# Hymba block (mLSTM and sparse attention heads) on one core: order of weight sums, gate evaluation, paced transposes and a block-by-block ending

## The chip, the cores and the metric

One Trainium2 core of a chip, one launch. The metric is device microseconds of that core. The engines: TensorE (PE, with its weight loads as PEld), VectorE (DVE), ScalarE (ACT), GpSimd (POOL) and the queue of SyncE (SP), which issues the loads of weights.

## What is computed

A batch of 256 tokens with 4096 features goes through one block in float32:

```
h = rmsnorm(x);  u = h @ w_in                       # 4096 x 15424
y_ml = rmsnorm(mlstm(conv(q,k), v, i, f)) * sigmoid(o) * silu(z)     # 8 heads
y_ns = (compressed + selected + window attention, gated) * silu(z)   # 16 heads
x = x + concat(y_ml, y_ns) @ w_out                  # 4096 x 4096
x = x + sigmoid(x @ ple_gate) * (p @ ple_proj)      # 4096 x 4096 and 256 x 4096
```

Nearly all of the work is three products of a 256-row matrix with weights that are read once.

## The kernel before

**Exact products by halves.** A float32 operand is split into hi (rounded to the type that TensorE multiplies fast) and lo (the rest). ScalarE makes hi (`whi`, L1235), VectorE makes lo (`wlo = raw - whi`, L1236). A product is three matmuls of 128x128 by 128x512: hi·hi, lo·hi, hi·lo. The activations are split likewise, transposed, into `sh` and `sl`, eight chunks of four blocks of 128 features.

**Units.** The program is a list of units. A unit takes one load of weights (512 KB, tile `raw`, six of them in flight at most), its split and its matmuls. The split of unit n+3 is issued ahead of the matmuls of unit n (LOOK = 3); there are four `whi` and four `wlo` tiles, so hi of unit n+3 can begin when unit n-1 has been multiplied. After each unit one `step()` runs one piece of side work from two queues of generators, first `urgent`, then `fifo`; `require(flag)` runs steps until a flag is set. All engines work through their instructions in the order in which this loop issues them.

**Phase 1** (`wide_group`) multiplies by `w_in` in 30 groups of 16 units of 12 matmuls, into two PSUM banks each, tags `mm0` and `mm1` with two buffers each. The last four groups are mo0 to mo3, whose results go through `t_mo`: a sigmoid out of PSUM (L673), a yield, then four multiplications into the activations (L679). During mo3, `t_stat` (L705) transposes a finished chunk (L713), splits it one step later into `sh`, `sl` (L724 to L730), and for some chunks builds mixed tiles `cb` (L738 to L747). Its last chunk follows in a second generator.

**Phases 2 and 3** (`pair_group`, groups 0 to 3 on `w_out`, 4 to 7 on `ple_gate`) make 256x1024 results of four accumulators `own[t][j]` (t half of the tokens, j half of the columns). Weights come in pairs of 256 rows, kp = 0 to 15. A plain pair C is two units of 12 matmuls, 8 products. A mixed pair is multiplied with 7 products (the Strassen-Winograd scheme): units a1 (3 matmuls, half a split), a2 (6), c1 (6), c2 (6). Its c units need sums of the two weight tiles, four additions on VectorE (L1105 to L1108), issued with the split of a2. `PLANS` orders the pairs: a few plain ones, then mixed pairs, each with a plain pair between its a and its c, then plain ones. One such period, a1 a2 C0 C1 c1 c2, is 45 matmuls. There are 5, 6, 6, 6, 4, 6, 6, 6 of them in the eight groups. In groups 4 to 7 two units P multiply `p` by `ple_proj` (L1153 to L1155); they need `ph`, `pl`, the split of `p` by `t_p` (L928, L929).

**Between groups 3 and 4** `t_stat` makes the activations of phase 3 from x1: chunks 0 and 1 in the last units of group 3, on the banks that group 4 then takes as its accumulators, chunks 2 to 7 after group 3, followed in `fifo` by `t_p`. Group 4 starts with `require("r1")` (chunk 1 split), its P units with `require("p")`.

**The end.** Group 7 ends with plain pairs 14 and 15. `t_out_own` takes each accumulator in two halves of 256 columns: add (L996), sigmoid (L997), multiply (L998), add (L999), and stores it from the SP queue (L1000).

Of the kernel before, what the change touches and what calls it, by code (L numbers as in the profile page):

```python
# [48 lines left out]
def _plan(head, mixed, between, tail):  # L49
# [9 lines left out]
    _plan((0, 1), MIXED, (2, 4, 6, 8, 10, 12), (14, 15)),  # L59
    _plan((0, 1), MIXED, (2, 4, 6, 8, 10, 12), (14, 15)),  # L60
    _plan((0,), MIXED, (1, 2, 4, 6, 8, 10), (12, 14, 15)),
    _plan((0, 1, 2, 3, 4), (), (), ()) + PROJ + _plan((5,), (7, 9, 11, 13), (6, 8, 10, 12), (14, 15)),
] + [_plan((0,), (), (), ()) + PROJ + _plan((1,), MIXED, (2, 4, 6, 8, 10, 12), (14, 15))] * 3


# [8 lines left out]
def hymba_block(ctx: ExitStack, tc: tile.TileContext, a, out: bass.AP):  # L74
    nc = tc.nc
# [591 lines left out]
        done.add(flag)  # L667
        yield

    def t_mo(ps, flag, j):  # L670
        u = utile([128, 2, 512])
        for t in range(2):
            nc.scalar.activation(u[:, t], ps[t], AF.Sigmoid, scale=rt[:, t:t + 1])  # L673
        done.add(flag)
        yield
        for t in range(2):
            for h in (2 * j, 2 * j + 1):
                yc = nat[h // 4][:, t, (h % 4) * 256:(h % 4) * 256 + 256]
                nc.vector.scalar_tensor_tensor(yc, yc, rr[:, t, h:h + 1], u[:, t, (h % 2) * 256:(h % 2) * 256 + 256],  # L679
                                               op0=OP.mult, op1=OP.mult)  # L680
        yield
# [20 lines left out]
            t = held["cb"][:, int(kp == 11)]  # L702
        return t[:, 0], t[:, 1]

    def t_stat(chunks, weighted, bset=1):  # L705

        def trans(c, col0, gate, flag):
            src, o = nat[col0 // 1024], col0 % 1024
            pp = [bank(bset, 2 * (c % 2) + half, [128, 2, 256]) for half in range(2)]
            for i in range(4):  # L710
                for t in range(2):
                    k = o + i * 128
                    nc.tensor.transpose(pp[i // 2][:, i % 2, t * 128:(t + 1) * 128], src[:, t, k:k + 128], idn)  # L713
            return pp

        def split(pp, c, col0, gate, flag):
            new_stat(c)
            for half in range(2):
                p = pp[half]
                if col0 // 128 in weighted:  # L720
                    for i in range(2):
                        k = 2 * half + i
                        wc = hnw[:, col0 // 128 + k:col0 // 128 + k + 1]
                        nc.scalar.activation(sh[c][:, k], p[:, i], AF.Copy, scale=wc)  # L724
                        nc.vector.scalar_tensor_tensor(sl[c][:, k], p[:, i], wc, sh[c][:, k],
                                                       op0=OP.mult, op1=OP.subtract)
                else:
                    hs = slice(2 * half, 2 * half + 2)
                    nc.scalar.activation(sh[c][:, hs], p, AF.Copy)
                    nc.vector.tensor_sub(sl[c][:, hs], p, sh[c][:, hs])  # L730
                kp = 2 * c + half
                if kp in MIXED:

                    f = stile([128, 4, 128])
                    if col0 // 128 in weighted:
                        for i in range(2):
                            k = col0 // 128 + 2 * half + i
                            nc.scalar.activation(f[:, 2 * i:2 * i + 2].rearrange("p a t -> p (a t)"), p[:, i], AF.Copy,  # L738
                                                 scale=hnw[:, k:k + 1])
                    else:  # L740
                        nc.scalar.activation(f.rearrange("p a t -> p (a t)"), p.rearrange("p a t -> p (a t)"), AF.Copy)
                    nc.vector.tensor_sub(f[:, 3:0:-2], f[:, 1::-1], f[:, 3:0:-2])
                    nc.vector.tensor_sub(f[:, 0], f[:, 0], f[:, 3])
                    nc.vector.tensor_sub(f[:, 2], f[:, 2], f[:, 0])
                    cb[kp] = mixed_tiles(kp)
                    nc.scalar.activation(cb[kp][0], f, AF.Copy)
                    nc.vector.tensor_sub(cb[kp][1], f, cb[kp][0])  # L747
            done.add(flag)

        last = None  # L750
        for ch in chunks:
            while ch[2] not in done:
                yield
            pp = trans(*ch)
            if last:
                split(*last)
            last = (pp, *ch)
            yield
        split(*last)
        yield  # L760

# [73 lines left out]
    def p1_post(name):  # L835
# [3 lines left out]
        def post(ps, flag):  # L839
# [18 lines left out]
            elif kind == "mv":  # L858
                urgent.append(t_mv(ps, flag, i))
                if i == 3:  # L860
                    add(t_mlstm(1))
            elif kind == "mz":
                add(t_mz(ps, flag, i))
                if i == 1:
                    add(t_mlstm(0))
            elif kind == "mo":
                add(t_mo(ps, flag, i))
                ch = [(c, (c * 512 + 2048) % 4096, f"p1_{c}", f"y{c}") for c in range(8)]
                if i == 2:
                    add(t_stat(ch[:7], range(16)))  # L870
                if i == 3:
                    add(t_stat(ch[7:], range(16)))
# [114 lines left out]
    def t_out_own(g, own, us, pj):  # L987
# [3 lines left out]
        if g == 7:  # L991
            for j in range(2):
                for t in range(2):
                    for c in (slice(0, 256), slice(256, 512)):
                        w = us[j][:, t, c]
                        nc.vector.tensor_add(w, own[t][j].t[:, c], w)  # L996
                        nc.scalar.activation(w, w, AF.Sigmoid)  # L997
                        nc.vector.tensor_tensor(w, w, pj[:, j, t, c], op=OP.mult)  # L998
                        nc.vector.tensor_add(w, w, x1[:, t, 512 - 512 * j + c.start:512 - 512 * j + c.stop])  # L999
                    nc.sync.dma_start(out[t * 128:(t + 1) * 128, 3584 - 512 * j:4096 - 512 * j], us[j][:, t])  # L1000
            done.add("own7")
            return
        for j in range(2):
# [19 lines left out]
    def pair_group(g, w, stat):  # L1023
# [2 lines left out]
        nC, nM = (sum(1 for kind, _ in plan if kind == x) for x in "Ca")  # L1026
        own = [[Acc(6 * nC + (0 if (t, j) == (1, 0) else 3 * nM)) for j in range(2)] for t in range(2)]
        oth = [Acc(3 * nM) for _ in range(4)]
        us, pj, raw, left = [], {}, {}, {c: 2 for c in range(8)}

        def start():
            require("ev_mo2" if g == 0 else f"oth{g - 1}")
# [20 lines left out]
        def product(acc, st, hi, lo):  # L1053
            return [(acc, st[0], hi), (acc, st[1], hi), (acc, st[0], lo)]

        def mixed(kp, i):
            return cb[kp][0][:, i], cb[kp][1][:, i]

# [17 lines left out]
                    first_a[0] = False  # L1076
            units.append(dict(src=src, mm=mm, pre=pre, post=post, kind="pair", split=split))

        def c_unit(kp, k, last):
            def mm(hi, lo):  # L1080
                bl = blocks(kp)
                if last and g == 7:
                    for j in range(2):
                        for t in range(2):
                            emit(product(own[t][j], bl(k, t), hi[:, j], lo[:, j]))
                    return
                for j in range(2):
                    emit([p for ps in zip(*(product(own[t][j], bl(k, t), hi[:, j], lo[:, j]) for t in range(2))) for p in ps])

            def post():  # L1090
                if k:
                    finish(kp)
            unit(w[kp, k], lambda r: split_all(r), mm, kp, post=post)

        def a_units(kp):
            def split1(r):
# [1 line left out]
                return split_one(r)  # L1098

            def split2(r):  # L1100
                r0 = raw[kp][0]
                raw[kp].append(r)
                hl = split_all(r, keep=True)

                nc.vector.tensor_add(r0[:, 1], r0[:, 1], r0[:, 0])  # L1105
                nc.vector.tensor_add(r0[:, 0], r0[:, 0], r[:, 0])
                nc.vector.tensor_add(r[:, 0], r[:, 0], r0[:, 1])
                nc.vector.tensor_add(r[:, 1], r[:, 1], r[:, 0])  # L1108
                return hl

            def mm1(hi, lo):
                emit(product(oth[0], blocks(kp)(0, 0), hi[:, 0], lo[:, 0]))

            def mm2(hi, lo):
                emit(product(own[0][0], mixed(kp, 2), hi[:, 0], lo[:, 0]))
                emit(product(own[0][1], blocks(kp)(1, 0), hi[:, 1], lo[:, 1]))
            unit(w[kp, 0], split1, mm1, kp, True)
            unit(w[kp, 1], split2, mm2, kp)

        def c_units(kp, last):  # L1120
            def mm1(hi, lo):
                emit(product(oth[3], mixed(kp, 1), hi[:, 0], lo[:, 0]))
                emit(product(oth[1], mixed(kp, 3), hi[:, 1], lo[:, 1]))

            def mm2(hi, lo):
                emit(product(oth[2], mixed(kp, 0), hi[:, 0], lo[:, 0]))
                emit(product(own[1][1], blocks(kp)(1, 1), hi[:, 1], lo[:, 1]))

            def post():
                finish(kp)  # L1130
                if last:
                    urgent.append(t_x1_oth(g, oth) if g < 4 else t_out_oth(g, oth, us))
                    if g == 3:
                        add(t_stat([(c, c * 512, f"p2_{c}", f"r{c}") for c in range(2)], (), 0))
            unit(None, lambda _: split_all(raw[kp][0]), mm1)
            unit(None, lambda _: split_all(raw[kp][1]), mm2, post=post)

# [30 lines left out]
        marks = max(i for i, (kind, _) in enumerate(plan) if kind == "c")  # L1168
        for i, (kind, kp) in enumerate(plan):
            if kind == "C":  # L1170
                c_unit(kp, 0, False)
                c_unit(kp, 1, i == len(plan) - 1)
            elif kind == "a":
                a_units(kp)
            elif kind == "c":
# [15 lines left out]
        def end():  # L1191
# [4 lines left out]
            else:  # L1196
                urgent.append(t_out_own(g, own, us, pj[0]))
            if g == 3:
                add(t_stat([(c, c * 512, f"p2_{c}", f"r{c}") for c in range(2, 8)], ()), t_p())
        units[-1]["post"] = end  # L1200

    for g in range(4):
# [183 lines left out]
```

## Time and profile before

| what | us |
|---|---|
| time, median of 3 runs | 2217.81 (2217.38 to 2218.21) |
| the profiled execution's own time | 2219.09 |
| its span, first to last instruction | 2217.3 |

The profiled execution is 1.28 us above the median; 1.79 us of it lie outside the span. Times in the rows below count from the start of the span. TensorE's matmuls overlap: each is listed with some 0.39 us, but one can start every 0.23 us, so the step from start to start tells the rate, and a busy TensorE is not yet one at its rate.

### The profile page before, as it was taken

What the parts mean: (1) busy time and instruction counts of PE and PEld (TensorE: products, weight loads), DVE (VectorE), ACT (ScalarE), POOL (GpSimd) and SP (SyncE); (2) the same over time, 40 slices, a digit from 0 to 9 for tenths busy, and PEclk for the clock granted to TensorE, in tenths of its full rate; (3) what the DMA queues carried; (4) which work ended last, traced back from release to release, by engine and by line L of the source; (5) the groups of instructions that cost most, each with busy time, mean ns of one, the idle gap of its engine ahead of it and who ended that gap; (6) DMA issues with size and microseconds to landing.
All of it is one profiled execution on the core that took longest, in us unless ns stands there. A gap on an engine that the chain in (4) does not pass through costs nothing.

```text
span 2217.3 us, 26509 instructions
## 1 busy us (share of the span) xinstructions
PE 2173.1 (98%) x9885; PEld 1773.4 (80%) x9885; DVE 1399.3 (63%) x1735; ACT 1093.0 (49%) x1376; POOL 32.2 (1%) x70
## 2 busy tenths in 40 slices
PE   9999999999999999999999999979999999999997
PEld 7876888888888888888888888867877877778785
DVE  6553554555655555745564455568888887888887
ACT  7543443555544454444444445455455555555553
POOL 1000000000000000000000000000000000000000
PEclk9999999999999999999999999989999999999998
DMA  9567555555555454655566555555555563656653
GB/s 378 198 200 262 185 191 185 181 158 167 169 161 171 160 178 143 193 194 183 180 193 194 191 182 181 180 188 197 200 191 189 209 209 131 218 180 212 226 191 114
DMA packets 118097, 422.05 MB, mean 190 GB/s; under 512 B 13634, under 2 KB 13690, under 8 KB 117968
## 3 DMA queue, kind: packets, MB, share of 16 engines
q1 hardware_dynamic: 114128, 409.00, 55.4%
q0 software_dynamic: 3696, 11.35, 1.6%
q8 instruction: 77, 1.26, 0.2%
q14 instruction: 52, 0.43, 0.1%
q10 hardware_dynamic: 144, 0.02, 0.0%
HBM read 416.08 MB, written 4.23 MB: 190 GB/s over the span
## 4 chain that ended last, share of the span: by engine, by line
PE 88%; DVE 6%; ACT 4%; issue 1%; DMA 0%; SPq 0%; ACTq 0%; DVEq 0%
PE mm L800 39%; PE mm L802 19%; PE mm L1020 11%; PE sd L1020 11%; DVE wlo L1236 4%; ACT whi L1235 4%; PE sd L540 1%; PE sd L910 1%; DVE raw L1105 1%; PE sd L543 1%; PE sd L529 0%; PE sd L237 0%; DVE sl L730 0%; PE sd L452 0%; DMA raw<-in_w_in 0%
## 5 line engine op out<-in xcount | busy, mean ns | idle before, releaser
L1236 DVE TENSOR_TENSOR wlo<-raw,whi 128x1024 fp32r<-128x1024 f32 x788 | 952.1, 1224 | 721.6 <-ACT whi L1235 716.4
L1235 ACT ACTIVATE whi<-raw 128x1024 fp32r<-128x1024 f32 x788 | 829.6, 1059 | 915.3 <-PE mm L800 574.6
L800 PE MATMUL mm<-whi,sh 128*128 128x512 f32 x1920 | 603.7, 396 | 0.3 <-ACT whi L1235 0.3
L800 PE MATMUL mm<-whi,sl 128*128 128x512 f32 x1920 | 592.5, 390 | 0.0
L802 PE MATMUL mm<-wlo,sh 128*128 128x512 f32 x1920 | 592.0, 389 | 0.1
L802 PEld LDWEIGHTS mm<-wlo,sh 128*128 128x128 f32 x1920 | 360.4, 188 | 76.7 <-DVE wlo L1236 0.5
L800 PEld LDWEIGHTS mm<-whi,sl 128*128 128x128 f32 x1920 | 360.4, 188 | 76.4
L800 PEld LDWEIGHTS mm<-whi,sh 128*128 128x128 f32 x1920 | 352.2, 188 | 77.8 <-issue 5.5
L1020 PE MATMUL mm<-whi,sh 128*128 128x512 f32 x410 | 134.2, 395 | 14.7 <-ACT u L673 12.4
L1020 PE MATMUL mm<-wlo,sh 128*128 128x512 f32 x410 | 134.8, 397 | 3.4 <-DVE wlo L1236 3.3
L1020 PE MATMUL mm<-whi,sl 128*128 128x512 f32 x410 | 132.7, 392 | 0.0
L1020 PE MATMUL sd<-wlo,sh 128*128 128x512 f32 x389 | 128.2, 396 | 3.9 <-DVE wlo L1236 3.9
L1020 PE MATMUL sd<-whi,sh 128*128 128x512 f32 x389 | 126.1, 390 | 0.0
L1020 PE MATMUL sd<-whi,sl 128*128 128x512 f32 x389 | 125.9, 390 | 0.0
L1020 PEld LDWEIGHTS mm<-whi,sh 128*128 128x128 f32 x410 | 77.0, 189 | 32.0 <-ACT u L673 12.8
L1020 PEld LDWEIGHTS mm<-wlo,sh 128*128 128x128 f32 x410 | 76.1, 189 | 26.1 <-DVE wlo L1236 11.0
L1020 PEld LDWEIGHTS sd<-wlo,sh 128*128 128x128 f32 x389 | 71.5, 188 | 26.2 <-DVE wlo L1236 12.4
L1020 PEld LDWEIGHTS mm<-whi,sl 128*128 128x128 f32 x410 | 77.6, 189 | 16.5
L1020 PEld LDWEIGHTS sd<-whi,sl 128*128 128x128 f32 x389 | 73.0, 188 | 15.5
L1020 PEld LDWEIGHTS sd<-whi,sh 128*128 128x128 f32 x389 | 72.9, 188 | 15.5
L1242 ACT ACTIVATE whi<-raw 128x512 fp32r<-128x512 f32 x45 | 28.5, 633 | 69.5 <-PE sd L1020 34.0
L1020 PE MATMUL mm<-whi,cb 128*128 128x512 f32 x186 | 57.5, 390 | 0.0
(293 smaller groups left out, 1415.5 us busy)
## 6 DMA issues: line engine op xcount, KB each, us to landing
raw<-in_w_in SPq DMA_DIRECT2D x479, 512.0 KB, 3.5
raw<-in_w_out SPq DMA_DIRECT2D x128, 512.0 KB, 4.8
raw<-in_ple_gate SPq DMA_DIRECT2D x128, 512.0 KB, 4.6
raw<-in_w SPq DMA_DIRECT2D x16, 512.0 KB, 3.6
u<-in_xt SPq DMA_DIRECT2D x16, 256.0 KB, 7.7
xn<-in_x SPq DMA_DIRECT2D x4, 1024.0 KB, 9.3
x<-in_x POOLq DMA_DIRECT2D x4, 1024.0 KB, 9.3
raw<-in_ple_proj SPq DMA_DIRECT2D x8, 512.0 KB, 4.8
```

The source lines that it names most:

```text
L540: MM(o[t][:, h, :], ptb[i][:, b, s, :], v[:, s, b, g * 128:(g + 1) * 128], start=(b == 0 and s == 0), stop=False)
L543: MM(o[t][:, h, :], pct[32 * h:32 * h + NCMP, t, :], vcmp[32 * h:32 * h + NCMP, g, :], start=False, stop=True)
L800: MM(box["ps"][t], s[c][:, k, t * 128:(t + 1) * 128], m[:, j, :], start=st, stop=False)
L802: MM(box["ps"][t], sh[c][:, k, t * 128:(t + 1) * 128], lo[:, j, :], start=False, stop=last)
L910: MM(o[64 * kv:64 * kv + 60], xq[l // 8][:, l % 8, 60 * kv:60 * kv + 60], raw[:, j, 256 * kv:256 * kv + 256], start=(l == 0), stop=(l == 31))
L1020: MM(acc.t, s, m, start=acc.i == 0, stop=acc.i == acc.n - 1)
L1105: nc.vector.tensor_add(r0[:, 1], r0[:, 1], r0[:, 0])
L1235: nc.scalar.activation(hi, r, AF.Copy)
L1236: nc.vector.tensor_sub(lo, r, hi)
L1242: nc.scalar.activation(hi[:, 0], r[:, 1], AF.Copy)
```

## The change

Five parts:

1. The four additions on the tiles of a mixed pair move from the split of a2 into the splits of the plain pair behind it: two after the split of C0, two after the split of C1. The products of a2, c1 and c2 are issued alternately for both accumulators (`both`), so that lo is used from the fifth matmul on, not the third.
2. `t_mo` is cut in two. The sigmoid becomes `t_mo_gate` on `urgent`, the multiplications stay on `fifo`.
3. `t_stat` gets a `pace`: after each chunk it yields that many times. It is 2 between groups 3 and 4, and 1 in phase 1 as before.
4. Group 4 has seven plain pairs ahead of its P units instead of five, and pair 7 becomes plain: three mixed pairs instead of four.
5. In group 7 the four units of pairs 14 and 15 issue nothing until the last one, and then their 48 matmuls block by block: the accumulators of j = 0 first. The stores follow each block; whole blocks of 512 columns for the first three, halves for the last.

```diff
-    _plan((0, 1, 2, 3, 4), (), (), ()) + PROJ + _plan((5,), (7, 9, 11, 13), (6, 8, 10, 12), (14, 15)),
+    _plan((0, 1, 2, 3, 4, 5, 6), (), (), ()) + PROJ + _plan((7,), (9, 11, 13), (8, 10, 12), (14, 15)),
...
-    def t_mo(ps, flag, j):
-        u = utile([128, 2, 512])
+    def t_mo_gate(ps, flag, j):
+        u = held[f"mo{j}"] = utile([128, 2, 512])
         for t in range(2):
             nc.scalar.activation(u[:, t], ps[t], AF.Sigmoid, scale=rt[:, t:t + 1])
         done.add(flag)
         yield
+
+    def t_mo(j):
+        u = held[f"mo{j}"]
...
             last = (pp, *ch)
-            yield
+            for _ in range(pace):
+                yield
...
-                add(t_mo(ps, flag, i))
+                urgent.append(t_mo_gate(ps, flag, i))
+                add(t_mo(i))
...
-                    for c in (slice(0, 256), slice(256, 512)):
-                        w = us[j][:, t, c]
-                        nc.vector.tensor_add(w, own[t][j].t[:, c], w)
-                        nc.scalar.activation(w, w, AF.Sigmoid)
+                    cs = (slice(0, 256), slice(256, 512)) if t and j else (slice(0, 512),)
+                    for c in cs:
+                        nc.vector.tensor_add(us[j][:, t, c], own[t][j].t[:, c], us[j][:, t, c])
+                        nc.scalar.activation(us[j][:, t, c], us[j][:, t, c], AF.Sigmoid)
+                    for c in cs:
+                        w, c0 = us[j][:, t, c], 512 - 512 * j + c.start
+                        n = c.stop - c.start
                         nc.vector.tensor_tensor(w, w, pj[:, j, t, c], op=OP.mult)
-                        nc.vector.tensor_add(w, w, x1[:, t, 512 - 512 * j + c.start:512 - 512 * j + c.stop])
-                    nc.sync.dma_start(out[t * 128:(t + 1) * 128, 3584 - 512 * j:4096 - 512 * j], us[j][:, t])
+                        nc.vector.tensor_add(w, w, x1[:, t, c0:c0 + n])
+                        nc.sync.dma_start(out[t * 128:(t + 1) * 128, 3072 + c0:3072 + c0 + n], w)
...
+        def both(*products):
+            emit([p for ps in zip(*products) for p in ps])
...
+        def sums(kp, k):
+            r0, r = raw[kp]
+            if k == 0:
+                nc.vector.tensor_add(r0[:, 1], r0[:, 1], r0[:, 0])
+                nc.vector.tensor_add(r0[:, 0], r0[:, 0], r[:, 0])
+            else:
+                nc.vector.tensor_add(r[:, 0], r[:, 0], r0[:, 1])
+                nc.vector.tensor_add(r[:, 1], r[:, 1], r[:, 0])
+        def c_unit(kp, k, last, opened=None):
+            def split(r):
+                hl = split_all(r)
+                if opened is not None:
+                    sums(opened, k)
+                return hl
...
+                if last:
+                    tail.append((bl, k, hi, lo))
+                    if len(tail) < 4:
+                        return
+                    order = [(t, j) for j in range(2) for t in range(2)]
+                    seq = [(b, i) for b in order[0:2] for i in range(3)] + [(b, 3) for b in order[0:2]]
+                    for (t, j), i in seq + [(b, i) for b in order[2:4] for i in range(4)]:
+                        bl, k_, hi, lo = tail[i]
+                        emit(product(own[t][j], bl(k_, t), hi[:, j], lo[:, j]))
                     return
...
             def split2(r):
                 raw[kp].append(r)
-                hl = split_all(r, keep=True)
-                nc.vector.tensor_add(r0[:, 1], r0[:, 1], r0[:, 0])
-                nc.vector.tensor_add(r0[:, 0], r0[:, 0], r[:, 0])
-                nc.vector.tensor_add(r[:, 0], r[:, 0], r0[:, 1])
-                nc.vector.tensor_add(r[:, 1], r[:, 1], r[:, 0])
-                return hl
+                return split_all(r, keep=True)
...
-                        add(t_stat([(c, c * 512, f"p2_{c}", f"r{c}") for c in range(2)], (), 0))
+                        add(t_stat([(c, c * 512, f"p2_{c}", f"r{c}") for c in range(2)], (), 0, 2))
...
+                opened = plan[i - 1][1] if i and plan[i - 1][0] == "a" else None
+                for k in range(2):
+                    c_unit(kp, k, g == 7 and i >= len(plan) - 2, opened)
...
-                add(t_stat([(c, c * 512, f"p2_{c}", f"r{c}") for c in range(2, 8)], ()), t_p())
+                add(t_stat([(c, c * 512, f"p2_{c}", f"r{c}") for c in range(2, 8)], (), 1, 2), t_p())
```

## Rows read from the trace of the kernel before

**Rows 1.** Page, part 1: engine, busy us (share of the span), instructions.
```profile
PE 2173.1 (98%) x9885; PEld 1773.4 (80%) x9885; DVE 1399.3 (63%) x1735; ACT 1093.0 (49%) x1376; POOL 32.2 (1%) x70
```
**Rows 2.** Page, part 6: loads of weights, count, size, median us from issue to landing.
```profile
raw<-in_w_out SPq DMA_DIRECT2D x128, 512.0 KB, 4.8
```
**Rows 3.** TensorE's waits: who waited for whom, us in total, times, longest.
```profile
PE sd L1020 <- DVE wlo L1236: 3.9, 20, 0.2
PE mm L1020 <- DVE wlo L1236: 3.3, 17, 0.2
```
**Rows 4.** Stretches: length, busy us of PE, PEld, DVE, ACT, POOL, clock, DMA.
```profile
1462.80:1481.00 18.20, 5.83 (x15) 4.24 (x15) 10.96 (x21) 9.66 (x16) 0.00 (x0) 0.62 0.33 103
...
1508.93:1519.63 10.70, 10.49 (x47) 8.37 (x46) 9.05 (x10) 5.83 (x6) 0.00 (x0) 1.00 0.39 131
```
**Rows 5.** Timeline of one period, group 0: start us, us, what, [idle before].
```profile
1508.93 1.23 DVE L1236 TENSOR_TENSOR wlo<-raw,whi 128x1024 fp32r<-128x1024 f32 x1 [2.45 <-ACT whi L1235]
1509.42 1.06 ACT L1235 ACTIVATE whi<-raw 128x1024 fp32r<-128x1024 f32 x1 [0.53 <-PE sd L1020]
...
1510.07 0.68 DVE L1105 TENSOR_TENSOR raw<-raw 128x512 f32<-128x512 f32 x1
...
1512.86 4.62 DVE L1236 TENSOR_TENSOR wlo<-raw,whi 128x1024 fp32r<-128x1024 f32 x4
...
1513.31 0.61 PE L1020 MATMUL mm<-whi,sl 128*128 128x512 f32 x2
1514.13 0.74 PE L1020 MATMUL mm<-wlo,sh 128*128 128x512 f32 x2 [0.21 <-DVE wlo L1236]
...
1519.63 1.23 DVE L1236 TENSOR_TENSOR wlo<-raw,whi 128x1024 fp32r<-128x1024 f32 x1 [1.55 <-ACT whi L1235]
```
**Rows 6.** Chain that ended last, plain units between periods: start us, us, what.
```profile
1650.41 10.88 PE mm L1020 x48
```
**Rows 7.** Timeline from phase 1 to phase 2, as rows 5.
```profile
1456.52 1.03 PE L713 MATMUL sd<-idn,y 128*128 128x128 f32 x8
...
1467.13 0.46 ACT L724 ACTIVATE sh<-sd,hnw_c 128x256 fp32r<-128x256 f32 x1
...
1474.89 1.25 ACT L673 ACTIVATE u<-mm,rt 128x512 f32<-128x512 f32 x2
...
1475.61 0.79 PE L1020 MATMUL mm<-whi,sh 128*128 128x512 f32 x1 [12.37 <-ACT u L673]
```
**Rows 8.** ScalarE's timeline where the first sigmoid of `t_mo` now stands.
```profile
1364.90 1.28 ACT L673 ACT_TABLE_LOAD   x1
```
**Rows 9.** Timeline from group 3 to the P units of group 4.
```profile
1825.56 1.28 DVE L730 TENSOR_TENSOR sl<-mm,sh 128x512 fp32r<-128x512 f32 x2
...
1827.52 0.50 PE L1020 MATMUL mm<-whi,sh 128*128 128x512 f32 x1 [0.66 <-ACT s L741]
...
1828.79 1.03 PE L713 MATMUL sd<-idn,x 128*128 128x128 f32 x8
1829.21 1.04 ACT L1235 ACTIVATE whi<-raw 128x1024 fp32r<-128x1024 f32 x1
...
1835.08 1.05 ACT L1235 ACTIVATE whi<-raw 128x1024 fp32r<-128x1024 f32 x1
...
1863.06 0.50 PE L1153 MATMUL sd<-whi,ph 128*128 128x512 f32 x1
...
1865.01 0.50 PE L1154 MATMUL sd<-whi,pl 128*128 128x512 f32 x1 [1.44 <-DVE pl L929]
```
**Rows 10.** Timeline of the end.
```profile
2200.51 0.42 DVE L996 TENSOR_TENSOR u<-sd,u 128x256 f32<-128x256 f32 x1 [4.48 <-PE sd L1020]
...
2202.12 0.39 PE L1020 MATMUL sd<-wlo,sh 128*128 128x512 f32 x1
2202.22 0.42 DVE L996 TENSOR_TENSOR u<-sd,u 128x256 f32<-128x256 f32 x1
...
2213.85 0.42 DVE L999 TENSOR_TENSOR u<-u,x 128x256 f32<-128x256 f32 x1
```

More of the change, by code (lines that the diff above doesn't have):

```diff
@@ L703, in mixed_tiles, with t_stat @@
         return t[:, 0], t[:, 1]
-    def t_stat(chunks, weighted, bset=1):
+    def t_stat(chunks, weighted, bset=1, pace=1):
         def trans(c, col0, gate, flag):
@@ L1028, in pair_group @@
         oth = [Acc(3 * nM) for _ in range(4)]
-        us, pj, raw, left = [], {}, {}, {c: 2 for c in range(8)}
+        us, pj, raw, left, tail = [], {}, {}, {c: 2 for c in range(8)}, []
         def start():
@@ L1077, in unit @@
             units.append(dict(src=src, mm=mm, pre=pre, post=post, kind="pair", split=split))
-        def c_unit(kp, k, last):
+        def sums(kp, k):
[12 more added lines that the diff above has]
+                return hl
             def mm(hi, lo):
                 bl = blocks(kp)
[L1082 to L1085, printed above, removed]
+                if last:
[7 more added lines that the diff above has]
+                        emit(product(own[t][j], bl(k_, t), hi[:, j], lo[:, j]))
                     return
                 for j in range(2):
-                    emit([p for ps in zip(*(product(own[t][j], bl(k, t), hi[:, j], lo[:, j]) for t in range(2))) for p in ps])
+                    both(*(product(own[t][j], bl(k, t), hi[:, j], lo[:, j]) for t in range(2)))
             def post():
@@ L1092, in post @@
                     finish(kp)
-            unit(w[kp, k], lambda r: split_all(r), mm, kp, post=post)
+            unit(w[kp, k], split, mm, kp, post=post)
         def a_units(kp):
@@ L1100, in split2 @@
             def split2(r):
-                r0 = raw[kp][0]
                 raw[kp].append(r)
-                hl = split_all(r, keep=True)
-                nc.vector.tensor_add(r0[:, 1], r0[:, 1], r0[:, 0])
-                nc.vector.tensor_add(r0[:, 0], r0[:, 0], r[:, 0])
-                nc.vector.tensor_add(r[:, 0], r[:, 0], r0[:, 1])
-                nc.vector.tensor_add(r[:, 1], r[:, 1], r[:, 0])
-                return hl
+                return split_all(r, keep=True)
             def mm1(hi, lo):
@@ L1114, in mm2 @@
             def mm2(hi, lo):
-                emit(product(own[0][0], mixed(kp, 2), hi[:, 0], lo[:, 0]))
-                emit(product(own[0][1], blocks(kp)(1, 0), hi[:, 1], lo[:, 1]))
+                both(product(own[0][0], mixed(kp, 2), hi[:, 0], lo[:, 0]),
+                     product(own[0][1], blocks(kp)(1, 0), hi[:, 1], lo[:, 1]))
             unit(w[kp, 0], split1, mm1, kp, True)
@@ L1121, in mm1 @@
             def mm1(hi, lo):
-                emit(product(oth[3], mixed(kp, 1), hi[:, 0], lo[:, 0]))
-                emit(product(oth[1], mixed(kp, 3), hi[:, 1], lo[:, 1]))
+                both(product(oth[3], mixed(kp, 1), hi[:, 0], lo[:, 0]),
+                     product(oth[1], mixed(kp, 3), hi[:, 1], lo[:, 1]))
             def mm2(hi, lo):
-                emit(product(oth[2], mixed(kp, 0), hi[:, 0], lo[:, 0]))
-                emit(product(own[1][1], blocks(kp)(1, 1), hi[:, 1], lo[:, 1]))
+                both(product(oth[2], mixed(kp, 0), hi[:, 0], lo[:, 0]),
+                     product(own[1][1], blocks(kp)(1, 1), hi[:, 1], lo[:, 1]))
             def post():
@@ L1170, in pair_group @@
             if kind == "C":
-                c_unit(kp, 0, False)
-                c_unit(kp, 1, i == len(plan) - 1)
+                opened = plan[i - 1][1] if i and plan[i - 1][0] == "a" else None
+                for k in range(2):
+                    c_unit(kp, k, g == 7 and i >= len(plan) - 2, opened)
             elif kind == "a":
```

## The prediction

> **What bounds the kernel now.** I read the page's engine line first: TensorE is busy for 2173.1 of 2217.3 us [rows 1]. So a change can gain only where TensorE waits, or where the span goes on without it. The list of its waits looks poor, 37 waits on `wlo` for 7.2 us together [rows 3], but it counts only what lies behind the listed end of a matmul, and matmuls overlap. The step from start to start tells more: 48 matmuls of plain units take 10.88 us, 0.227 each [rows 6], so a unit of 12 takes 2.72 and a period of 45 should take 10.2. In the timeline a period takes 10.70, from the split at 1508.93 to its like at 1519.63 [rows 5]. Inside it, the pair of matmuls at 1513.31 should be followed at 1513.76; the next comes at 1514.13, 0.37 late, and itself takes 0.11 more than its neighbours before the one after it starts [rows 5]. It is C0's first use of lo. VectorE has that lo late because it does a2's lo (1508.93), then four additions from 1510.07, and only at 1512.86 C0's lo, whose hi was ready at 1510.48 [rows 5]. This happens in 37 of the 45 periods, all but the first of each group [rows 3].
>
> The other places outside the rate: 12.4 us at the start of phase 2, on the sigmoid of mo3 [rows 7]; some 7 us between group 3 and the P units [rows 9]; and the end, where the last matmul starts at 2202.12 and the last addition ends at 2214.27 [rows 10].
>
> **Part 1, the sums: -17.8 us.** Take as zero 1507.84, where a2's hi starts (1.06 and a hand-over ahead of its lo at 1508.93). lo of a2 ends at 2.3. With no additions in front, C0's lo follows its hi (ends at 2.64) and ends at 3.9; it is needed at 5.9. Two additions of 0.68 and 0.04 hand-over each [rows 5] run to 5.3, C1's lo to 6.5 (needed at 8.6), two more additions to 7.9, c1's lo to 9.1 (needed at 11.4 with the alternating order), c2's to 10.2 (needed at 12.7). Every one keeps 2 us. The additions are not gone, they lie in VectorE's slack: it is busy for 9.05 of 10.70 [rows 4], which is 89% of 10.2. Removed: 0.37 + 0.11 in 37 periods, 17.8 us. Bounds: nothing, if the wait moves to the next lo, and 18.5 by the whole difference 10.70 - 10.2. I take the value read at the place.
>
> What the moved additions hold up: C1's `raw` is released at 6.5 rather than 7.4, c1's at 9.1 rather than 8.5, and the next loads wait for these on SP. A load lands in 4.8 [rows 2]. That of the next C1 is used 6.6 after its issue: covered by 1.8. The alternating order by itself gives nothing once lo is early; 0, between -1 and +1.
>
> **Part 2, the urgent sigmoid: nothing.** The 12.4 us end when the sigmoid of mo3 frees a bank (1474.89), and I count what stands ahead of it on ScalarE. The transposes at 1456.52 are chunk 6, issued after unit 13 of mo3: two units, 5.4 us, follow before phase 2 tries to start. The step after unit 13 also splits chunk 5, the one after unit 14 splits chunk 6 (from 1467.13), the one after unit 15 was the first piece of `t_mo`, since the generator of chunks 0 to 6 had ended and `t_mo` of mo3 was the next in `fifo`. Now the step after unit 15 takes the same sigmoid from `urgent`. It has the same place on ScalarE, behind the same splits, whose ping-pong with VectorE is what is late. `pace` stays 1 there. [...]
>
> What does move is the sigmoid of mo0, from 1364.90 to some 40 us earlier, into the exponentials of `t_mlstm`. That adds two table loads of 1.28 [rows 8] and moves 1.25 us of sigmoid: 3.8 us of ScalarE, which is busy 49% [rows 1]. The look-ahead of three units, 8.2 us less 2.3 for hi and lo, hides it: 0, at most +1. [...]
>
> **Parts 3 and 4, group 3 to group 4: -2.8 us.** Before, from 1828.79 to 1863.06 there are 9 units (24.5 us) and six times 8 transposes (listed 1.03, some 0.88 from start to start, 5.3 us): 4.5 us of 34.3 are idle [rows 9]. Cause: with one chunk per unit ScalarE and VectorE hand each other hi, lo and mixed tiles in a loop of 5.87 us (1829.21 to 1835.08 [rows 9]), while TensorE needs 3.6. With pace 2 it is one chunk per two units, 6.3 us of TensorE against about 6.9 (5.87 and one more hi). Five chunks with mixed tiles fall some 3 us behind, which the look-ahead hides. Seven plain pairs give 14 steps: 13 for six chunks and the last split, the 14th for the load of p. So -4.5; at the worst none of it.
>
> Against it stand three costs. (a) Pair 7 plain: 24 matmuls for 21, +0.7. (b) Step 14 is the load, so `ph` and `pl` are only issued by the `require("p")` of the first P unit, behind hi and lo of a unit three ahead. hi can start 0.25 before TensorE gets there; 0.94, then lo 1.14 on VectorE, then `pl` 0.69: ready 2.7 after, a wait of 2.45. Before it was 1.72 (1863.06 to 1865.01 less one step [rows 9]) and 0.17 ahead of it. +0.6, between -1.9 and +2. (c) With pace 2 the second yield eats the step that transposed chunk 1, and the last unit's step goes to `urgent`; so `require("r1")` issues chunk 1's transposes and both splits at once ahead of group 4. TensorE arrives 0.9 earlier, VectorE has chunk 0's two differences (1.28 [rows 9]) more to do before chunk 1 frees the last bank, which ended the wait at 1827.52: +0.4, between 0 and +2.
>
> **Part 5, the end: -7.2 us.** Before, eight halves run one after the other, 1.71 us each (2200.51 to 2202.22 [rows 10]), as each addition stands behind the multiplication before it, which waits for the sigmoid. Let T = 2202.51 be the last matmul's end. In the new order the blocks are complete at T-6.1, T-5.4, T-2.7 and T. A whole block costs 0.71 add, 0.64 sigmoid, 0.71 multiply, 0.6 to the next: 2.66 (0.68 per operation [rows 5], 0.63 [rows 7]). Three of them from T-6.1 end at T+1.9; the last block's halves overlap, add, sigmoid, multiply, add and one more pair of half steps: 2.6. T+4.5, where it was T+11.8 [rows 10]. The store after it is taken as before. Bounds: -9 if the first blocks never hold up the last, -5 if they start 2 us late. Holding back three units costs TensorE nothing: the fourth split is needed 18 matmuls, 4.1 us, after the first, and is made within 2.8.
>
> **Sum:** -17.8 + 0 - 4.5 + 0.7 + 0.6 + 0.4 - 7.2 = -27.8. The profiled execution's 2219.09 becomes 2191.3; the median of the runs lies 1.28 lower: 2190.0.
>
> **The rivals.**
> - *The sigmoid's wait goes* (part 2 works): 2190.0 - 14.6 = 2175.4. For it: the wait is named after that very line. Against: the count of steps. 5%.
> - *Half of the period's wait comes back at the next lo*, if VectorE's hand-overs are longer than I reckon: 8.9 us of 17.8 stay, 2198.9. Against: 2 us of slack at each. 9%.
> - *The burst ahead of group 4* costs more than (b) and (c) say, with TensorE idle until a slow restart as at phase 2: 6 us more, 2196. 4%.
> - *Slower: VectorE becomes the bound of every period.* Each lo must wait for its hi, each hi for a tile that TensorE frees; with additions between the splits VectorE would stand still in front of C1, c1 and c2. The place is the splits of C0 and C1 in 44 periods. At 2.2 us of standing beside its 9.05 a period takes 11.25: 44 x 0.55 = +24, with -7.2 and -2.8 it is +14, 2232. It decides from 10.93 on (10.0 / 44 over 10.70), 1.9 us of standing. For it: 89% busy. Against: hi is ready ahead of VectorE in all but C0's and a2's case, which cost 0.4. 3%.
>
> **How the numbers follow.** The forecast, 2186 to 2194 by itself, has 79%. The range 2184 to 2199 takes in the half-wait and the burst. A measurement of this kernel tells 0.2%, 4.4 us, from no change: faster 0.96, same 0.01, slower 0.03.
>
> **What would show it.** Step 1: 10.2 to 10.3 us from a2's lo to the next, no TensorE wait on `wlo` in the periods. Step 2: still 12 us on the sigmoid at the start of group 0; if that row is gone, my count of steps was wrong. Steps 3 and 4: no waits between group 4's chunks, some 2.5 us on `pl` at the first P unit, a wait at group 4's first unit no shorter than before. Step 5: the last addition 4.5 us after the last matmul. A period still at 10.7, or over, would make the whole prediction wrong.

## The result, and the profile after

| what | before | after |
|---|---|---|
| time, median (lowest to highest) | 2218.01 (2217.38 to 2218.43), 4 runs | 2193.43 (2191.79 to 2195.67), 4 runs |
| the profiled execution's own time | 2219.09 | 2191.79 |
| its span | 2217.3 | 2190.0 |

The ratio is 0.989 [0.9873, 0.9907]: 24.6 us less by the medians. A second series (x0 below), four runs against seven, gives 2194.01 against 2218.39, 0.989 [0.9873, 0.9906]. The forecast was 2190.0 in 2184 to 2199, so it came 3.4 us too low. The same sum takes the profiled span of 2217.3 to 2189.5, and it is 2190.0. So most of the 3.4 lies between one profiled execution, the shortest of the four, and the median. The last part of the section on the prediction says what the record shows of that.

Engine line of the page, as [rows 1]: TensorE is busy 11.7 us less, the span is 27.3 shorter.
```profile
PE 2161.4 (99%) x9888; PEld 1777.6 (81%) x9888; DVE 1397.7 (64%) x1720; ACT 1094.7 (50%) x1373; POOL 32.1 (1%) x70
```
TensorE's waits (who waited for whom, us in total, times, longest), as [rows 3]. All rows on `wlo` are gone; beside a wait of 2.7 at the program's start, which was there before, what stays is the sigmoid of mo3, one wait at group 4's start and two at the first P unit.
```profile
PE mm L1028 <- ACT u L673: 12.1, 1, 12.1
...
PE mm L1028 <- DVE sl L733: 2.6, 1, 2.6
PE sd L1179 <- ACT ph L933: 1.8, 1, 1.8
PE sd L1180 <- DVE pl L934: 1.6, 1, 1.6
```
Stretches (length, busy us of PE, PEld, DVE, ACT, POOL, clock, DMA share, GB/s), as [rows 4]: one period; the P units; group 4's start; phase 2's start.
```profile
1508.62:1518.82 10.20, 10.20 (x46) 8.45 (x45) 9.14 (x10) 5.84 (x6) 0.00 (x0) 1.00 0.56 180
1862.20:1869.80 7.60, 5.86 (x25) 4.63 (x26) 2.87 (x4) 2.35 (x5) 0.00 (x0) 1.00 0.61 209
1815.90:1821.10 5.20, 4.91 (x23) 3.68 (x24) 3.46 (x8) 2.18 (x3) 0.00 (x0) 1.00 0.38 102
1463.10:1481.00 17.90, 5.81 (x17) 4.32 (x16) 10.95 (x21) 9.66 (x16) 0.00 (x0) 0.62 0.32 102
```
The timeline of that period, as [rows 5]. C0's lo now follows its hi at once and ends at 1511.16; the additions come behind it, and TensorE's pairs on `whi` and `wlo` at 1512.95 and 1513.40 follow without a gap (0.45 is two steps).
```profile
1508.62 2.54 DVE L1263 TENSOR_TENSOR wlo<-raw,whi 128x1024 fp32r<-128x1024 f32 x2 [1.93 <-ACT whi L1262]
1508.84 1.06 ACT L1262 ACTIVATE whi<-raw 128x1024 fp32r<-128x1024 f32 x1 [0.25 <-PE sd L1028]
1511.08 0.68 DVE L1094 TENSOR_TENSOR raw<-raw 128x512 f32<-128x512 f32 x1
1511.80 0.69 DVE L1095 TENSOR_TENSOR raw<-raw 128x512 f32<-128x512 f32 x1
1512.41 1.22 DVE L1263 TENSOR_TENSOR wlo<-raw,whi 128x1024 fp32r<-128x1024 f32 x1
1512.95 0.61 PE L1028 MATMUL mm<-whi,sl 128*128 128x512 f32 x2
1513.40 0.62 PE L1028 MATMUL mm<-wlo,sh 128*128 128x512 f32 x2
...
1518.82 1.23 DVE L1263 TENSOR_TENSOR wlo<-raw,whi 128x1024 fp32r<-128x1024 f32 x1 [0.83 <-ACT whi L1262]
```
Phase 1 to phase 2, as [rows 7]: the last transposes before it, split 6, the sigmoid and the restart stand where they stood, within 0.3 us. The restart is slow in both: 9 matmuls come 0.43 apart, 11 before, and not 0.227; the granted clock from the first matmul to 1480.50 is 0.54, before 0.50.
```profile
1456.78 1.03 PE L716 MATMUL sd<-idn,y 128*128 128x128 f32 x8
...
1467.11 0.45 ACT L727 ACTIVATE sh<-sd,hnw_c 128x256 fp32r<-128x256 f32 x1
...
1474.86 1.25 ACT L673 ACTIVATE u<-mm,rt 128x512 f32<-128x512 f32 x2
...
1475.58 0.80 PE L1028 MATMUL mm<-whi,sh 128*128 128x512 f32 x1 [12.09 <-ACT u L673]
```
Group 3 to the P units, as [rows 9]. Two chunks of ScalarE's work are 7.01 apart; TensorE's two units and eight transposes are 6.33.
```profile
1844.91 1.03 PE L716 MATMUL sd<-idn,x 128*128 128x128 f32 x8
...
1847.52 0.60 ACT L744 ACTIVATE s<-sd 128x512 f32<-128x512 f32 x1 [1.71 <-DVE sl L733]
...
1851.24 1.03 PE L716 MATMUL sd<-idn,x 128*128 128x128 f32 x8
...
1854.53 0.60 ACT L744 ACTIVATE s<-sd 128x512 f32<-128x512 f32 x1 [1.71 <-DVE sl L733]
...
1861.61 0.63 ACT L933 ACTIVATE ph<-u 128x512 fp32r<-128x512 f32 x1
1862.29 0.49 PE L1179 MATMUL sd<-whi,ph 128*128 128x512 f32 x1 [1.84 <-ACT ph L933]
1863.69 0.69 DVE L934 TENSOR_TENSOR pl<-u,ph 128x512 fp32r<-128x512 f32 x1
1864.43 0.50 PE L1180 MATMUL sd<-whi,pl 128*128 128x512 f32 x1 [1.65 <-DVE pl L934]
```
The end, as [rows 10]: the first block is added at 2176.60, while TensorE still works on the others.
```profile
2176.60 0.69 DVE L1001 TENSOR_TENSOR u<-sd,u 128x512 f32<-128x512 f32 x1
...
2182.09 0.39 PE L1028 MATMUL sd<-wlo,sh 128*128 128x512 f32 x1
...
2184.76 0.75 DVE L1001 TENSOR_TENSOR u<-sd,u 128x256 f32<-128x256 f32 x2
...
2186.92 0.42 DVE L1007 TENSOR_TENSOR u<-u,x 128x256 f32<-128x256 f32 x1
```

### The profile page after: what moved, and what is told of

It is laid out like the page before. It is cut to its first block, busy times and chain, and to the rows that moved or that the text cites. A ratio compares the mean times of both kernels' runs of the same rounds, so it can differ in the third digit from the quotient of the medians.

```text
span 2190.0 us, 26498 instructions
## 1 busy us (share of the span) xinstructions
PE 2161.4 (99%) x9888; PEld 1777.6 (81%) x9888; DVE 1397.7 (64%) x1720; ACT 1094.7 (50%) x1373; POOL 32.1 (1%) x70
## 5 line engine op out<-in xcount | busy, mean ns | idle before, releaser
L1263 DVE TENSOR_TENSOR wlo<-raw,whi 128x1024 fp32r<-128x1024 f32 x787 | 961.9, 1224 | 707.2 <-ACT whi L1262 694.2
L1028 PE MATMUL mm<-whi,sh 128*128 128x512 f32 x416 | 135.6, 394 | 14.9 <-ACT u L673 12.1
L1028 PE MATMUL sd<-whi,cb 128*128 128x512 f32 x168 | 55.8, 390 | 0.0
```

What stands on the lines that cost most here:

```text
L1028: MM(acc.t, s, m, start=acc.i == 0, stop=acc.i == acc.n - 1)
L1263: nc.vector.tensor_sub(lo, r, hi)
```

## The experiments

Where one run is given, spans and places of the profiled executions are compared; the runs of one kernel lie 1 us (x1) to 4 us (the changed kernel) apart.

**x1: the sums alone** (the kernel before with part 1, without the alternating order).
```diff
-                hl = split_all(r, keep=True)
-                nc.vector.tensor_add(...)          # four of them
-                return hl
+                return split_all(r, keep=True)
+                opened = plan[i - 1][1] if i and plan[i - 1][0] == "a" else None
+                c_unit(kp, 0, False, opened)       # sums(opened, 0) behind its split
+                c_unit(kp, 1, i == len(plan) - 1, opened)
```


> The kernel before with part 1 alone, and of it only the place of the four additions (two behind each split of the plain pair); the products keep their old order. Theory (C0's lo was late because of the additions in front of it, 0.48 us in 37 periods): a period of 10.2 us, no TensorE wait on wlo in the periods, 2217.8 - 17.8 = 2200.0. Rival 1 (half of the wait comes back at the next lo, which without the alternating order is used 0.45 us earlier in c1 and c2): period 10.45, 2209. Rival 2 (VectorE is the bound of a period): 10.7 or more, 2217 or above.

Measured: 2200.02 (2199.49 to 2200.47) against 2219.01, ratio 0.9914 [0.9897, 0.993], so 19.0 us less. The period is at the rate:
```profile
1508.60:1518.80 10.20, 10.20 (x47) 8.45 (x46) 9.13 (x10) 5.83 (x7) 0.00 (x0) 1.00 0.56 183
```
What follows: the place of the four additions, by itself, makes two thirds of the gain by the profiled spans (18.6 of 27.3 us) and three quarters by the medians (19.0 of 24.6).

**x2: the sums back** (the changed kernel, additions in a2's split again).
```diff
-                if opened is not None:
-                    sums(opened, k)
...
-                return split_all(r, keep=True)
+                hl = split_all(r, keep=True)
+                sums(kp, 0)
+                sums(kp, 1)
+                return hl
```


> The changed kernel with the four additions back in the split of a2, all else as changed. Theory: the wait of 0.48 us at C0's lo is back in 36 periods (three mixed pairs in group 4), +17.3 us against the changed kernel: span 2190.0 + 17.3 = 2207. Rival (the alternating order alone hides the wait, since lo of a2 is used later): below 2195.

Measured: 2212.47 in one run, span 2210.7. The period is 10.70 again, and the waits are back (36 for 36 periods; there is one period less than before):
```profile
PE sd L1028 <- DVE wlo L1264: 4.0, 20, 0.2
PE mm L1028 <- DVE wlo L1264: 3.2, 16, 0.2
```
The timeline has C0's lo at 1512.00 behind four additions, and the next pair on `wlo` late as in [rows 5]:
```profile
1512.00 4.62 DVE L1264 TENSOR_TENSOR wlo<-raw,whi 128x1024 fp32r<-128x1024 f32 x4
...
1513.27 0.73 PE L1028 MATMUL mm<-wlo,sh 128*128 128x512 f32 x2 [0.21 <-DVE wlo L1264]
```
What follows: 18.1 us above x0's span of 2192.6, which restarts slowly at the P units as x2 does, with 11 matmuls 0.43 apart in both. The two stretches with periods, from the first matmul of phase 2 to the first transposes for phase 3 (352.89, in x0 343.34) and from the P units' end to the last matmul's (321.05, in x0 312.71), are 17.9 longer, 0.50 in each of 36 periods. The rest is not the additions' doing: x2 has 0.9 more in a slow restart at group 4's start and came to phase 2 0.7 earlier. The listed waits hold only 7.2 of the 17.9.

**x9: the old order of products** in a2, c1 and c2 (lo from the third matmul on); plain units stay as changed.
```diff
-            emit([p for ps in zip(*products) for p in ps])
+            for p in products:
+                emit(p)
```


> The changed kernel with the products of a2, c1 and c2 one after the other again (lo used from the third matmul, not the fifth); plain units as they are. Theory (once the additions are out of the way every lo is 2 us early): periods 10.2 us, no wait on wlo, span that of the changed kernel, 2190 plus 0, 2.5 or 5 for slow restarts. Rival (the alternating order carries part of the gain): waits on wlo in c1 or c2, periods of 10.4 or more.

Measured: 2194.38 in one run, span 2192.6; periods of 10.20, no wait on `wlo`:
```profile
1508.60:1518.80 10.20, 10.20 (x47) 8.45 (x46) 9.13 (x11) 5.83 (x6) 0.00 (x0) 1.00 0.51 177
```
What follows: the alternating order brings nothing that can be measured; early lo is enough.

**x3: the sigmoid in `fifo`.**
```diff
-                urgent.append(t_mo_gate(ps, flag, i))
-                add(t_mo(i))
+                add(t_mo_gate(ps, flag, i), t_mo(i))
```


> The changed kernel with the sigmoid of mo0 to mo3 back in fifo, in front of its multiplications, as before. Theory (the urgent queue leaves the sigmoid of mo3 at its old place): span 2190 within 1 us, wait on the sigmoid at the start of phase 2 12.1 us in both. Rival (urgent does shorten that wait, by the 0.3 us that it differs, or more): wait longer than 12.4 us, span 2191 or more.

Measured: 2194.42 in one run, span 2192.7. The wait is what it was:
```profile
PE mm L1027 <- ACT u L673: 12.3, 1, 12.3
```
Phase 2 goes on at 1475.36 (after: 1475.58). Of the span's 2.7 us over after's, 2.5 lie in the P units, 9.98 for 7.49, with 11 matmuls 0.43 apart. What follows: part 2 brings nothing, and its two table loads more (31 for 29) cost nothing that shows: the first transposes for phase 3 start at 1806.01 in after and at 1806.20 here.

**x4: fewer splits ahead of the sigmoid.** The late splits of phase 1 go to the second generator, behind `t_mo_gate`.
```diff
-                    add(t_stat(ch[:7], range(16)))
+                    add(t_stat(ch[:5], range(16)))
-                    add(t_stat(ch[7:], range(16)))
+                    add(t_stat(ch[5:], range(16), 1, 2))
```


> The changed kernel with chunks 5 and 6 of phase 1 taken out of the first t_stat and put into the second, behind the sigmoid of mo3, at pace 2 as between groups 3 and 4. Theory (the sigmoid waits on ScalarE for the splits of chunks 5 and 6): the wait at the start of phase 2 falls from 12.1 to 1 to 3 us and the slow restart (2.4 us) goes with it: 10 to 13 us off, 2193.4 - 11.5 = 2182. Rival 1 (the sigmoid is late for another reason, such as its own group's end or a table load): wait still 12 us, 2193. Rival 2 (the splits that move into group 0 hold up its first periods as much as they held up its start): wait gone, but 8 to 12 us of new waits in group 0, 2191 to 2195.

Measured: 2187.30 (2186.41 to 2188.80) against 2219.01, ratio 0.9858 [0.9843, 0.9873]: 6 us better than the change, where 11.5 were expected. The wait on the sigmoid is 0.3, but three others have come:
```profile
PE mm L1028 <- ACT whi L1262: 3.0, 2, 2.3
...
PE mm L804 <- ACT whi L1262: 1.2, 1, 1.2
PE mm L1028 <- ACT u L673: 0.3, 1, 0.3
```
After the 2.3 TensorE restarts slowly, with a granted clock of 0.74 in the stretch:
```profile
1494.00:1500.50 6.50, 4.24 (x13) 3.36 (x13) 5.39 (x8) 4.16 (x7) 0.00 (x0) 0.74 0.47 158
```
What follows: the splits ahead of the sigmoid on ScalarE were the cause of the 12.1, as the count of steps in the prediction had it. The 12 us were also a time in which ScalarE and VectorE went on with their splits; without it, about half of the gain is waited for in phase 1's last units and group 0: the first transposes for phase 3 start 7.1 earlier (1798.94 for 1806.01), not 14. That the wait had served as time to catch up is read from the new waits on `whi`, not tested by itself.

**x5: the end's order undone** (operations as changed, matmuls of the last units as before).
```diff
-                    c_unit(kp, k, g == 7 and i >= len(plan) - 2, opened)
+                    c_unit(kp, k, False, opened)
```


> The changed kernel with the matmuls of the last four units in the old manner (every unit at once, so that the accumulators of j = 0 end 1.4 us before the last matmul and those of j = 1 with it); t_out_own stays as changed, whole blocks first. Theory (7.2 us of the end are 2.5 from fewer and overlapping operations and 4.7 from blocks that are complete early): last addition 9.2 to 9.5 us after the last matmul's end instead of 4.9, span +4.4. Rival (the order matters little, the operations alone shorten the end): last addition 5 to 6 us after, span +1 or less.

Measured: 2197.03 in one run, span 2195.27. The last matmul ends at 2183.42, the last addition starts at
```profile
2192.18 0.42 DVE L1007 TENSOR_TENSOR u<-u,x 128x256 f32<-128x256 f32 x1
```
and ends 9.2 after the last matmul; the change has 4.9, before had 11.8. From last matmul to the end of the span: 14.81 before, 11.85 here, 7.54 after. What follows: 3.0 us come from whole blocks with fewer, less serial operations, 4.3 from the order of the matmuls. The 3.0 are, if anything, too few: the last unit before went block by block, here it alternates between the halves of the tokens, so the first addition starts 1.55 ahead of the last matmul's end (2181.87) and not 2.00 [rows 10].

**x6: parts 3 and 4 undone** (pace 1, the old plan of group 4).
```diff
-    _plan((0, 1, 2, 3, 4, 5, 6), (), (), ()) + PROJ + _plan((7,), (9, 11, 13), (8, 10, 12), (14, 15)),
+    _plan((0, 1, 2, 3, 4), (), (), ()) + PROJ + _plan((5,), (7, 9, 11, 13), (6, 8, 10, 12), (14, 15)),
-                        add(t_stat([...range(2)], (), 0, 2))
+                        add(t_stat([...range(2)], (), 0))
-                add(t_stat([...range(2, 8)], (), 1, 2), t_p())
+                add(t_stat([...range(2, 8)], ()), t_p())
```


> The changed kernel with pace 1 everywhere and the old plan of group 4 (parts 3 and 4 undone). Theory 1 (read from the profile after: parts 3 and 4 gained 4.1 us between chunks and gave back 3.3 at group 4's start, the P units and by pair 7): the idle time between chunks is back, the wait ahead of the first P unit is under 2 us and TensorE keeps its full clock through the P units; span 2190 to 2192. Theory 2 (they gained the 2.8 us of the prediction): span 2192.8 or more. Rival (the wait for ph and pl and a slow restart behind it cost more than pace 2 gains): span 2188 to 2190.

Measured: 2191.44 in one run, span 2189.7, no longer than the change; the rival of the expectation had 2188 to 2190. Its waits are shorter and more:
```profile
PE mm L1028 <- DVE sl L733: 1.6, 1, 1.6
PE sd L716 <- DVE sl L733: 1.2, 1, 1.2
PE mm L1028 <- ACT s L744: 0.7, 1, 0.7
PE sd L1180 <- DVE pl L934: 0.6, 1, 0.6
PE sd L716 <- ACT s L744: 0.6, 1, 0.6
```
What follows: parts 3 and 4 together bring nothing that stands clear of the restarts. From the first transposes for phase 3 to the last matmul's end this run takes 377.35, with two short slow restarts of 4 and 5 matmuls; after takes 376.47 with none, x0 378.98 with one of 11. They trade many short waits for three longer ones.

**x7: `p` split early.** `t_p`'s two pieces run in steps that pace 2 leaves idle, not after the last chunk.
```diff
-                add(t_stat([...range(2, 8)], (), 1, 2), t_p())
+                def t_stat_p(stat=t_stat([...range(2, 8)], (), 1, 2), p=t_p()):
+                    for i, _ in enumerate(stat):
+                        if i in (1, 3):
+                            next(p)
+                        yield
+                add(t_stat_p())
```


> The changed kernel with the split of p (ph, pl) issued in an idle step between chunks 2 and 3, not by require at the first P unit. Theory (in most executions of the changed kernel the 3.9 us of waiting there is followed by a restart at half clock, 2.5 us more; the profile after shows the wait without it, 7.5 us of P units, the runs x2, x3, x4 with it, 10.0): P units in 5.5 to 6 us at granted clock 1.00, 2193.4 - 3.9 - 2.5 = 2187 in the median, and a spread of the runs near that of the kernel before, 1 us. Rival 1 (the spread has another cause): 2189.5 and still 3 to 4 us of spread. Rival 2 (ph and pl hold two of the three s tiles and slow the mixed tiles of the later chunks): new waits between chunks, 2190 or more.

Measured: 2188.45 (2187.51 to 2189.91) against 2219.09, ratio 0.9861 [0.9845, 0.9877]. The P units take 5.44, as 24 matmuls at 0.227 do; group 4's start is slow in this execution:
```profile
1815.80:1821.10 5.30, 5.21 (x12) 4.01 (x13) 3.43 (x7) 1.62 (x3) 0.00 (x0) 0.50 0.30 99
1862.48:1867.92 5.44, 5.44 (x25) 4.51 (x24) 4.77 (x6) 4.23 (x7) 0.00 (x0) 1.00 0.79 256
```
What follows: 5 us by the medians lie in the waits at the P units and what follows them, where 6.4 were expected. The other place, group 4's start, remains, and so does a spread of 2.4 us, where 1 was expected.

**x8: three mends together**, x7 with the first generator of phase 3 at pace 1 and phase 1's splits cut at 5 (pace 1).
```diff
-                    add(t_stat(ch[:7], range(16)))
+                    add(t_stat(ch[:5], range(16)))
-                    add(t_stat(ch[7:], range(16)))
+                    add(t_stat(ch[5:], range(16)))
-                        add(t_stat([...range(2)], (), 0, 2))
+                        add(t_stat([...range(2)], (), 0))
```


> The changed kernel with x7's early split of p, chunks 0 and 1 between the groups at pace 1 again, and the splits of phase 1's chunks 5 to 7 behind the sigmoid of mo3 as in x4, but at pace 1, so that ScalarE is through with them before the first mixed pair of group 0 (in x4 it was not: 3.3 us of waits and a slow restart there). Theory: 2193.4 - 6.4 (x7) - 0.6 (group 4's start) - 10 to 12 (start of phase 2) = 2175 to 2177. Rival (three splits in a row hold up group 0's plain units by what is gained): 2180 to 2183.

Measured: 2178.21 (2176.77 to 2178.62) against 2219.09, ratio 0.9815 [0.9801, 0.983]. It is the best of all, 15 us below the change, and its waits are
```profile
PE mm L1028 <- DVE sl L733: 1.6, 1, 1.6
PE mm L804 <- ACT whi L1267: 1.2, 1, 1.2
PE sd L1028 <- ACT whi L1274: 0.7, 1, 0.7
PE mm L1028 <- ACT s L744: 0.7, 1, 0.7
PE mm L1028 <- ACT u L673: 0.3, 1, 0.3
```
What follows: the difference to x7 is 10.2 us by the medians, for the wait on the sigmoid and the wait at group 4's start together (11.6 by the profiled spans). The traces part them. The first transposes for phase 3, ahead of which only the splits of phase 1 differ, start 10.0 earlier than in x7 (first line x7, second x8); from there to the P units' end x8 takes 60.38, x7 61.99, so 1.6 lie at group 4's start.
```profile
1805.93 1.04 PE L716 MATMUL mm<-idn,x 128*128 128x128 f32 x8
1795.90 1.03 PE L716 MATMUL mm<-idn,x 128*128 128x128 f32 x8
```
No wait in group 0 is over 0.7 here, and TensorE's slow restart there is gone (clock 1.00 from 1481.00 to 1500.00). The sum of the expectation, 2175 to 2177, was 1 to 3 us too low.

**x0: the changed kernel again**, unchanged, in more runs.

> The changed kernel itself, once more, for its spread. Theory (after the waits at group 4's start and at the first P unit TensorE restarts at half clock in some executions and not in others, some 2.5 us each): times between 2191.5 and 2197, up to 5 us apart, the profiled one with as many slow restarts at these two places as its time lies multiples of 2.5 us above 2191.8. Rival (the spread has another cause): the profiled execution's time does not go with the number of slow restarts in its trace.

Measured: 2194.01 (2193.36 to 2194.49). Its profiled execution, at 2194.35, has the same two waits at the P units as after's, but restarts slowly: 11 matmuls come 0.43 apart, and the stretch has clock 0.66 where after has 1.00.
```profile
1862.30:1872.40 10.10, 8.38 (x25) 6.43 (x26) 2.86 (x4) 2.34 (x5) 0.00 (x0) 0.66 0.47 155
```
What follows: two executions of one kernel differ by 2.6 us of span, and 2.5 of that lie in this stretch (9.98 for 7.49).

## Why the prediction was right, and where it was off

The spans by places, before to after: phase 2's restart until the first transposes for phase 3, 340.41 to 330.43; from there to the end of the P units, 54.33 to 63.77, where four units of 2.72 more lie in front of the P units, so 52.89; from there to the last matmul's end, 332.16 to 312.70, with the four units 323.58; and the end, 14.81 to 7.54. That is -9.98, -1.44, -8.58 and -7.27, together -27.3. The sum of the forecast, -27.8, comes so near by luck in part: the stretches with the sums gave 1.4 more than forecast and parts 3 and 4 gave 2.0 less. It is also luck which execution was profiled: x0's, of the same kernel, has a span of 2192.6.

**Part 1** was forecast at -17.8 and pair 7 at +0.7. The first and third stretch hold -18.6 with pair 7 in them, so -19.2 for the sums. The mechanism is shown by x1 and x2: the additions stood in front of C0's lo, and VectorE's slack takes them behind it. The term was read 0.48 a period at the place; the whole period gives 10.70 - 10.20 = 0.50, 18.5 in 37. Of the 0.7 that is left, 0.4 is not of this part: behind the wait on the sigmoid 11 matmuls come 0.43 apart before, 9 after. The last 0.3 was not followed. The alternating order was put at 0, and x9 has 0. VectorE at 9.14 of 10.20 did not become the bound.

**Part 2** was forecast at 0 with the wait in its place. The sigmoid starts at 1474.86 (it was 1474.89 [rows 7]), x3 without part 2 waits as long, and x4 removes the wait by removing the splits counted ahead of it. So the count was right. The price put on the wait's end, 14.6, was too high: x4 gets 6 to 7 of it, and x8 gets 10 at that place. It was 12.4 for the wait [rows 7] and 2.2 for the slow restart behind it; the 2.2 no run shows as such. In before's trace thirteen steps take 5.51 there, from 1475.61 to 1481.12, and at 0.227 would take 2.95: 2.6.

**Parts 3 and 4** were forecast at -2.8; the second stretch gives -1.44, and with pair 7's +0.7 it is -0.8. This is the step that was mis-sized, and mostly in term (b), the first P unit. The prediction put its wait at 2.45 against 1.89 before, from the assumption that ScalarE starts the P unit's hi 0.25 before TensorE gets there. It also had chunks falling 3 us behind, hidden by the look-ahead, and missed that the lag is still there at this place. The chunk loop takes 7.01 of ScalarE's and VectorE's hand-overs against 6.33 of TensorE, so `ph` starts only at 1861.61. TensorE waits 1.84 for `ph` and 1.65 for `pl`; with what lies behind the listed ends, 3.9. x7 takes both away: its P stretch is 5.44, so 2.05 of after's 7.49 were `pl`. (b) was +2.0 instead of +0.6. Term (c), group 4's start, was +0.4 and is +0.8: the listed wait is 2.58 there, and the third set of transposes, behind the same 36 matmuls, starts 13.55 after the first where it was 12.77. The idle time between the chunks gave some 4.2 for the 4.5 forecast.

**Part 5** was forecast at -7.2 and gave -7.27. The last addition ends 4.86 after the last matmul (forecast 4.5), and x5 shares it out.

**From the profile to the median.** The forecast took the median to lie 1.28 under the profiled time, as before. It lies 1.64 above it: 2.9 of the 3.4 us. Behind TensorE's waits at group 4's start and at the P units comes a slow restart, matmuls 0.43 apart and not 0.227, in some executions and not in others, at 1 to 2.9 us each; the granted clock is 0.66 in x0's P units and 1.00 in after's, 0.50 at x7's start of group 4 and 1.00 at after's. The rival "burst" had the mechanism, at 4% and 6 us. Before has no such restart there in its profiled execution, and its waits are shorter [rows 9]; x1 and x6, with the same waits as before, have short ones of 4 to 7 matmuls, and x1's runs lie within 1.0 us. Of the profiled executions of kernels that keep both waits, after has none, x0 and x3 have one of 11 matmuls at the P units, and the others have one at each place: x2 5 and 11, x4 7 and 13, x5 8 and 5, x9 5 and 6. x8, which shortens one wait and removes the other, has 4 matmuls at group 4's start. A third place varies too: behind the 12 us on the sigmoid the restart has from 5 (x6) to 12 (x7) such matmuls, 1.4 us between them.

For the runs without a profile the record has the mean granted clock, and it falls as the time rises: 0.996, 0.995, 0.995 and 0.994 for the four of after from the shortest to the longest, 0.995, 0.995, 0.994 and 0.994 for x0's, 0.996, 0.996, 0.994 and 0.994 for x7's. The runs of before (0.993 to 0.995, 1.3 us apart) and of x1 (0.993 in all four, 1.0 us apart) show no such order. So the longer runs of the changed kernel had a lower granted clock on the mean; in which stretch no trace shows. What decides in one execution stays open; the rows show waits of equal length with either outcome: at the P units after has none of these matmuls and x0 has 11, behind waits of 1.84 and 1.65 in the one, 1.82 and 1.64 in the other.

## What to carry to other kernels

Read the step of a loop from start to start and look there for the instruction whose input is late: 7.2 us of listed waits were 18 us of time, and moving four additions behind the split that TensorE waited for was two thirds of the gain or more. When a long stall goes, price what it gave the other engines to catch up; here at least 4 and up to 8 of 14 us were lost again elsewhere. Pacing side work so that it runs in fewer, larger pieces was worth nothing here: the idle time between the pieces came back as longer waits around them, and in most profiled executions TensorE restarted slowly behind these. Look at the clock behind each wait, and in more than one profiled execution.

## What was not expected of the hardware

A stall of TensorE cost more than its length here, but not each time: behind the same two waits at the P units the next 24 matmuls took 7.49 us with the waits in one execution and 9.98 in another. In x9, two short slow restarts of 5 and 6 matmuls cost together what one of 11 costs in x0 (both spans 2192.6). Loads of `w_out` land in 3.6 us (median of 128) where they took 4.8 [rows 2], though as many bytes move in the same groups. It goes with the place of the additions: 3.6 in x1, which moves them alone, and 4.8 in x2, which puts them back; x8, which has them moved, has 4.0. That a different spread of the releases of `raw`, and so of the issues, is the reason is likely and was not tested.
